# The second product of a feed-forward block as seven block products in four PSUM banks

## The chip, the cores and the metric

The kernel runs on one core of a Trainium2 chip. The metric is device time in microseconds (us) of one execution. TensorE is PE, VectorE DVE, ScalarE ACT, GpSimd POOL and SyncE SP; SP issues most of the transfers.

## What is computed

One step of a two-layer decoder: attention and a recurrent branch, a layer norm, a feed-forward block, a layer norm. What matters here is the second half of a layer:

```python
x = LN(alpha * x + mix @ w_out, ln1_g, ln1_b)           # LN1
h = square(relu(x @ w_ff_up))                           # first product: 1024 -> 4096 features
x = LN(alpha * x + h @ w_ff_down, ln2_g, ln2_b)         # second product: 4096 -> 1024, LN2
```

There are 1056 tokens (1024 of a prompt, 32 of samples), 1024 model features and 4096 inner ones, all in float32.

## The kernel before

Features lie on the partitions, tokens along the free axis in three chunks of 384, 384 and 288 columns (`CH`, chunks 0, 1 and 2). A tile is 128 features by one chunk; the model has 8 such feature tiles (`KD`), the inner layer 32. Every float32 operand is split into two parts of PE's fast float32 form: hi, a rounded copy (ACT, L287 for tokens, L236 for weights), and lo, the rest (DVE, L288 and L237). A product of two tiles is three matmuls, hi by hi, lo by hi and hi by lo, all added up in one PSUM bank (`gemm_parts`, `products`, `mmul` L206).

PE's order is written out by hand around the layer norms (`manual_schedule`); elsewhere, and on all other engines, a scheduler orders the instructions by what they depend on, and every engine works through its queue in order. `book` puts the steps of a layer norm into an agenda, at offsets counted in modelled nanoseconds of PE work (`LN_TIMES`, `LN1_TIMES`), and `weave` and `due` let them run when PE's count of issued work has got there. A layer norm has three steps on PE: the mean (a matmul of ones by the sum of the 8 tiles), the variance, and the reciprocal root brought across the partitions (`rb`, `pr`).

`ff` runs a layer's feed-forward block:
- LN1 on each chunk, in turn with the last output tiles of the branch before it. In `layer_norm` a tile is scaled on DVE (L364), gets its bias on ACT (L370), is rounded to hi on ACT, and its lo part is a subtraction on POOL (L371). The normed tile is stored in `d_x` as the residual.
- The first product: four features tile by tile (`up`), then 14 pairs of features in seven block products for chunks 0 and 1 (`pair_up`; Strassen's scheme in Winograd's form). `sums_w` makes its sums of weights on POOL (L1392 to L1395). The squared features go to DRAM (`d_h`).
- The second product: 8 groups of four features. `features` loads and splits a group's tokens (12 tiles); for each of 8 output tiles and 3 chunks, `down` adds 12 matmuls in one bank, which DVE adds to a running sum in SBUF (L1469 for the first group, L1471 for the others). Four weight loads of 512 KB go with a group.
- The last group goes chunk by chunk in hand order; `add_up` (L313) sums the finished tiles of a chunk, six adds on POOL and the last on DVE, and LN2 of chunks 0 and 1 is booked into the work that follows; LN2 of chunk 2 runs at the end.

PSUM has pools `mm` (2 banks), `pb` (4, tag `b`) and `pc` (2, tag `c`). `outer` and `inner` hold the token tiles as slots by chunk (tiles `x` and `i`), `raw` and `w` weights before and after the split.

## Time and profile before

| | |
|---|---|
| time, median of 3 runs | 3560.16 us (3554.78 to 3564.04) |
| the profiled execution | 3554.68 us, span 3552.9 us, mean granted clock 0.975 |
| busy share of the span | PE 97%, DVE 58%, ACT 33%, POOL 29% |
| second product and LN2, layer 0 | some 1395 to 1776 us |
| second product and LN2, layer 1 | some 3142 to 3553 us, with the end of the kernel |

The busy share is an average over stages. What a change of one stage does is read from that stage: the windows give the busy time of each engine in a stretch, the PE timeline what PE waited for and how long (in brackets, with the instruction that released it). The granted clock is a share of full speed. A wait on an engine that isn't the last one to be ready costs nothing.

### The profile page before, as it was taken

The numbers are of one execution on the slowest core, as the hardware profiler recorded it, in microseconds if no ns is written. First come the engines' busy times: TensorE is split into PE (matmuls) and PEld (weight loads), VectorE is DVE, ScalarE is ACT, GpSimd is POOL, SyncE is SP. The second block draws the span as 40 slices with busy tenths as digits, with TensorE's granted clock in tenths as the row PEclk, the third lists the DMA queues.
The fourth block names the chain that finished last, engine by engine and source line by source line (L and its number), as shares of the span: only waits on it lengthen the run. The fifth ranks groups of instructions, "written<-read, shape, count | busy, mean of one in ns | idle before, by whom it ended". The sixth has DMA issues, their size and how long they took to land.

```text
span 3552.9 us, 65184 instructions
## 1 busy us (share of the span) xinstructions
PE 3433.6 (97%) x24950; PEld 3177.7 (89%) x24950; DVE 2077.5 (58%) x5308; ACT 1175.9 (33%) x2677; POOL 1014.6 (29%) x1318
## 2 busy tenths in 40 slices
...
GB/s 171 49 97 114 78 76 92 77 74 191 73 67 114 98 104 206 97 95 76 19 89 44 100 106 91 77 86 79 110 171 46 87 109 110 109 197 88 90 47 50
DMA packets 282360, 342.09 MB, mean 96 GB/s; under 512 B 111168, under 2 KB 244832, under 8 KB 282016
## 3 DMA queue, kind: packets, MB, share of 16 engines
...
q0 software_dynamic: 1536, 4.52, 0.3%
...
## 4 chain that ended last, share of the span: by engine, by line
PE 82%; DVE 4%; ACT 2%; issue 2%; POOL 2%; DMA 1%; SPq 0%; ACTq 0%; POOLq 0%; DVEq 0%
PE mm L206 35%; PE b L206 25%; PE c L206 20%; PE b L210 1%; DMA d_g<-gs 1%; PE b L792 1%; PE c L210 0%; DVE pd L1018 0%; DVE x L1293 0%; DMA x<-d_h 0%; POOL x L1293 0%; DVE ln L301 0%; ACT x L370 0%; DVE ln L300 0%; POOL x L371 0%
## 5 line engine op out<-in xcount | busy, mean ns | idle before, releaser
L206 PE MATMUL mm<-x,w 128*128 128x384 f32 (+1 forms) x6630 | 1326.8, 336 | 22.9 <-ACT x L287 7.2
L206 PEld LDWEIGHTS mm<-x,w 128*128 128x128 f32 x6630 | 1082.6, 191 | 81.1 <-issue 13.0
L237 DVE TENSOR_TENSOR w<-raw,w 128x1024 fp32r<-128x1024 f32 x260 | 336.9, 1296 | 248.3 <-ACT w L236 246.2
L236 ACT CAST w<-raw 128x1024 fp32r<-128x1024 f32 x260 | 273.1, 1050 | 589.6 <-PE b L206 367.2
L206 PE MATMUL b<-x,w 128*128 128x384 f32 (+1 forms) x1958 | 457.5, 320 | 0.9 <-DVE x L288 0.9
L206 PE MATMUL mm<-i,w 128*128 128x384 f32 (+1 forms) x2034 | 425.6, 329 | 27.9 <-ACT i L287 15.6
L206 PE MATMUL c<-i,w 128*128 128x384 f32 (+1 forms) x2080 | 421.8, 323 | 3.1 <-DVE i L1308 3.0
L206 PE MATMUL b<-i,w 128*128 128x384 f32 (+1 forms) x1570 | 391.5, 324 | 3.9 <-ACT i L287 3.9
L206 PEld LDWEIGHTS mm<-i,w 128*128 128x128 f32 x2034 | 348.9, 192 | 31.6 <-ACT i L287 15.8
L206 PEld LDWEIGHTS c<-i,w 128*128 128x128 f32 x2080 | 348.4, 188 | 5.8 <-DVE i L1308 3.7
L206 PEld LDWEIGHTS b<-x,w 128*128 128x128 f32 x1958 | 334.2, 188 | 1.4 <-DVE x L288 1.4
L206 PE MATMUL c<-x,w 128*128 128x384 f32 (+1 forms) x1424 | 310.5, 323 | 0.0
L206 PEld LDWEIGHTS b<-i,w 128*128 128x128 f32 x1570 | 276.4, 188 | 4.6 <-ACT i L287 4.6
L206 PEld LDWEIGHTS c<-x,w 128*128 128x128 f32 x1424 | 242.6, 190 | 0.3 <-DVE x L288 0.3
L313 POOL TENSOR_TENSOR i<-i,i 128x384 f32<-128x384 f32 (+1 forms) x36 | 35.4, 984 | 677.6 <-DVE i L1471 673.0
L820 POOL TENSOR_TENSOR z<-z,gs 128x384 f32<-128x384 f32 (+1 forms) x84 | 80.1, 954 | 293.3 <-issue 184.5
L1471 DVE TENSOR_TENSOR i<-i,b 128x384 f32<-128x384 f32 x144 | 74.9, 520 | 144.1 <-PE b L206 143.2
L1366 POOL TENSOR_TENSOR x<-x 128x384 f32<-128x384 f32 x112 | 112.9, 1008 | 143.0 <-ACT x L1365 137.5
L1365 ACT ACTIVATE x<-x 128x384 f32<-128x384 f32 x112 | 58.6, 523 | 241.0 <-DVE x L1433 152.4
L1099 POOL COPY sav<-vt 64x128 f32<-64x128 f32 x128 | 42.9, 335 | 333.1 <-PE c L206 302.0
L313 POOL TENSOR_TENSOR i<-i,x 128x384 f32<-128x384 f32 (+1 forms) x36 | 34.7, 964 | 281.3 <-DVE x L1324 274.9
L1112 POOL TENSOR_SCALAR sd<-S,eL 128x128 f32<-128x128 f32 x128 | 96.9, 757 | 49.1 <-DVE S L1136 46.3
...
## 6 DMA issues: line engine op xcount, KB each, us to landing
...
x<-d_h SPq DMA_DIRECT2D x128, 192.0 KB
...
```

The source lines that it names most:

```text
L206: return self.nc.tensor.matmul(out, lhsT=lhsT, rhs=rhs, start=start, stop=stop)
L210: self.nc.tensor.transpose(out, x, ident)
L236: nc.scalar.copy(wf[:, 0, :], raw)
L237: self.weng.tensor_tensor(wf[:, 1, :], raw, wf[:, 0, :].bitcast(F32), op=ALU.subtract)
L313: eng.tensor_tensor(sums[c].f, a, acc[k][c].f, op=ALU.add)
L792: nc.tensor.matmul(pG[:, :n], lhsT=gup[:, pr * 128:pr * 128 + 128], rhs=z[:, :n], start=True, stop=True)
L820: nc.gpsimd.tensor_tensor(out[:, :n], out[:, :n], prev[:, :n], op=ALU.add)
L1099: nc.gpsimd.tensor_copy(sav[Kk, :], vt[Kk, k // 2, :])
L1112: nc.gpsimd.tensor_scalar(sd, S0, ecol, None, op0=ALU.mult)
L1365: nc.scalar.activation(out=z.f, in_=z.f, func=AF.Relu)
L1366: P(z.f, z.f, z.f, op=ALU.mult)
L1471: nc.vector.tensor_tensor(a, a, p[:, :n], op=ALU.add)
```

## The change

`ff` is divided into `ff_up` and `ff_down`.

**The second product** takes the tokens of chunks 0 and 1, and the even and odd features, as a 2 by 2 matrix of blocks, and the weights of even and odd features by even and odd output tiles as another. Seven block products, in the order 1, 2, 5, 4, 6, 7, 3, give the four blocks of the result. Each product runs over all 16 feature pairs in 8 steps, in four PSUM banks, one for each pair of output tiles, and is drained once, by `done`. Chunk 2 (288 columns) rides along in products 1 and 2 and in 5 and 4, in four further banks, with no product saved. For a step, `prepare` loads two token blocks of a product (and two of chunk 2), and a weight block of 512 KB, or two in product 5, which are added on POOL (L1531, into `sk`, which stays); product 6 subtracts on POOL (L1534), 7 and 3 too (L1537), 128x1024 each. Jobs are prepared two ahead.

**The first product** keeps the squared features of a pair and stores, in place of 4 tiles of 384 and 2 of 288 columns, the 7 blocks of tokens that the second product wants (`quad`, three subtractions on POOL and one on DVE) and 3 blocks of chunk 2 (`third`, one on POOL). `sums_w` goes from POOL to DVE.

**Layer norms**: hi comes straight from ACT with the bias (L375), lo from one DVE instruction with the bias (L376); the residual is made and stored after that (L387). `LN1_TIMES` are smaller. LN2 of chunk 2 is booked at the start of product 6, of chunk 0 at the start of product 3; chunk 1 comes last, and so the next layer's attention takes its keys and queries in the order 0, 2, 1. Of LN2's sums, that of chunk 1 is made by `done` in the last two products.

```diff
-LN1_TIMES = [3000, 13500, 20000]
+LN1_TIMES = [2600, 11000, 15500]
...
-                nc.scalar.activation(out=a[k], in_=a[k], func=AF.Identity, bias=bk)
-                nc.scalar.copy(hi.t, a[k])
-                nc.gpsimd.tensor_tensor(lo.t, a[k], hi.f, op=ALU.subtract)
+                nc.scalar.activation(out=hi.t, in_=a[k], func=AF.Identity, bias=bk)
+                nc.vector.scalar_tensor_tensor(lo.t, a[k], bk, hi.f, op0=ALU.add, op1=ALU.subtract)
...
+        if keep is not None:
+            for k in range(KD):
+                nc.scalar.activation(out=a[k], in_=a[k], func=AF.Identity, bias=par[:, bcol + k:bcol + k + 1])
+                nc.sync.dma_start(out=keep[k, :, c0:c0 + n], in_=a[k])
...
+        def quad(k, b11, b12, b21, b22):
+            t1, t2, t4 = [get(0, F32) for _ in range(3)]
+            P(t1.f, b12.f, b11.f, op=ALU.subtract)
+            V(b12.f, b22.f, b12.f, op=ALU.subtract)
+            P(t2.f, b22.f, t1.f, op=ALU.subtract)
+            P(t4.f, t2.f, b21.f, op=ALU.subtract)
+            for t, z in ((1, b11), (5, t1), (7, b12), (3, b22), (6, t2), (2, b21), (4, t4)):
+                store(d_t[t - 1, k], z)
...
-            P(s[0], b[0], b[1], op=ALU.add)
-            P(s[1], s[0], a[0], op=ALU.subtract)
-            P(s[2], a[0], b[0], op=ALU.subtract)
-            P(s[3], a[1], s[1], op=ALU.subtract)
+            V(s[0], b[0], b[1], op=ALU.add)
+            V(s[1], s[0], a[0], op=ALU.subtract)
+            V(s[2], a[0], b[0], op=ALU.subtract)
+            V(s[3], a[1], s[1], op=ALU.subtract)
...
+        def weights(p, k):
+            raw = lambda q: self.wraw(i["w_down"][l, q, k])
+            if p in (1, 2, 4):
+                return self.wsplit(raw({1: 0, 2: 1, 4: 3}[p]))
+            if p == 5:
+                a, b = raw(2), raw(3)
+                sk[k] = keep.tile([128, 1024], F32, tag=f"s{k}", name=self.nm("sk"))
+                P(sk[k], a, b, op=ALU.add)
+                return self.wsplit(sk[k])
+            if p == 6:
+                P(sk[k], sk[k], raw(0), op=ALU.subtract)
+                return self.wsplit(sk[k])
+            a = raw(3 if p == 7 else 1)
+            P(a, a, sk[k], op=ALU.subtract)
+            return self.wsplit(a)
...
+        def done(p, mp, e, y):
+            m = 2 * mp
+            if p == 1:
+                u[mp] = self.outer.get(0)
+                nc.scalar.copy(u[mp].f, e)
+            elif p == 2:
+                add(residual(m, 0), e)
+                P(acc[m][0].f, acc[m][0].f, u[mp].f, op=ALU.add)
+                add(residual(m, 2), y)
+            elif p == 5:
+                add(residual(m, 1), e)
+                add(residual(m + 1, 1), e)
+            elif p == 4:
+                add(residual(m + 1, 0), e, -1.0)
+                add(residual(m + 1, 2), y)
+            elif p == 6:
+                V(u[mp].f, u[mp].f, e, op=ALU.add)
+                P(acc[m][1].f, acc[m][1].f, u[mp].f, op=ALU.add)
+            elif p == 7:
+                V(u[mp].f, u[mp].f, e, op=ALU.add)
+                V(acc[m + 1][0].f, u[mp].f, acc[m + 1][0].f, op=ALU.subtract)
+                P(acc[m + 1][1].f, acc[m + 1][1].f, u[mp].f, op=ALU.add)
+                u[mp].put()
+            else:
+                V(acc[m][1].f, acc[m][1].f, e, op=ALU.add)
+                V(sums[1].f, sums[1].f, acc[m][1].f, op=ALU.add)
...
+            for q, (p, k) in enumerate(jobs):
+                if q + 2 < len(jobs):
+                    ready.append(prepare(*jobs[q + 2]))
+                if k == 0:
+                    if p in (1, 5):
+                        y = fours()
+                    e = fours() if p in (6, 3) else [self.ps(self.pb, "b") for _ in range(4)]
+                if (p, k) == (6, 0):
+                    self.book(norm(2), LN_TIMES)
+                elif (p, k) == (3, 0):
+                    self.book(norm(0), LN_TIMES)
...
+                if k == 7:
+                    for mp in range(4):
+                        done(p, mp, e[mp][:, :n], y[mp][:, :n2])
+                    for c in {4: (2,), 7: (0,)}.get(p, ()):
+                        for m in range(KD):
+                            self.add_up(inner, sums, acc, m, c)
+                    if p == 7:
+                        sums[1] = inner.get(1)
+                        P(sums[1].f, acc[1][1].f, acc[3][1].f, op=ALU.add)
+                        for m in (5, 7):
+                            P(sums[1].f, sums[1].f, acc[m][1].f, op=ALU.add)
...
-        drain(norm(2, last=True))
+        drain(norm(1, last=True))
```

The order of instructions shows what this moves, at three places of layer 0. In the rows, `x` and `i` are token tiles (chunk, slot, number), `b`, `mm` and `c` PSUM banks.

DVE in the second product before: the drains L1471 stand one by one between the splits of weights and tokens, each for a bank of its own.

```order
L1471 TENSOR_TENSOR i_1_17_2789_15738<-i_1_17_2789_15738,c_17009 128x384
L1471 TENSOR_TENSOR i_2_0_2790_15739<-i_2_0_2790_15739,b_17023 128x288
L237 TENSOR_TENSOR w_17467<-raw_17465,w_17467 128x1024
L1471 TENSOR_TENSOR i_0_11_2791_15740<-i_0_11_2791_15740,mm_17042 128x384
L1471 TENSOR_TENSOR i_1_1_2792_15741<-i_1_1_2792_15741,b_17056 128x384
L1471 TENSOR_TENSOR i_2_1_2793_15742<-i_2_1_2793_15742,c_17070 128x288
L288 TENSOR_TENSOR i_0_10_3107_17557<-x_5_3105_17554,x_3_3106_17556 128x384
```

DVE after, at the seam between product 5 and product 4: the token splits L294 are those of product 4's second step, and L1557 are the drains of product 5.

```order
L243 TENSOR_TENSOR w_18067<-raw_18065,w_18067 128x1024
L294 TENSOR_TENSOR x_1_3259_17963<-x_9_3257_17960,x_15_3258_17962 128x384
L294 TENSOR_TENSOR x_6_3262_17969<-x_11_3260_17966,x_3_3261_17968 128x384
L294 TENSOR_TENSOR x_9_3265_17975<-x_5_3263_17972,x_15_3264_17974 128x288
L294 TENSOR_TENSOR x_6_3268_17981<-x_3_3266_17978,x_8_3267_17980 128x288
L1557 SCALAR_TENSOR_TENSOR i_0_11_3249_17936<-i_0_11_3249_17936,b_17325 128x384
L1557 SCALAR_TENSOR_TENSOR i_0_15_3250_17939<-i_0_15_3250_17939,b_17325 128x384
L1557 SCALAR_TENSOR_TENSOR i_0_16_3251_17942<-i_0_16_3251_17942,b_17326 128x384
L1557 SCALAR_TENSOR_TENSOR i_0_2_3252_17945<-i_0_2_3252_17945,b_17326 128x384
L1557 SCALAR_TENSOR_TENSOR i_0_3_3253_17948<-i_0_3_3253_17948,b_17327 128x384
L1557 SCALAR_TENSOR_TENSOR i_0_19_3254_17951<-i_0_19_3254_17951,b_17327 128x384
L1557 SCALAR_TENSOR_TENSOR i_0_18_3255_17954<-i_0_18_3255_17954,b_17328 128x384
```

The drains now stand together, two for each of the four banks, and behind the four splits.

POOL before, at the end of the second product: `add_up` for chunk 0 and the first of LN2's pair sums (L348).

```order
L313 TENSOR_TENSOR i_0_17_3319_18888<-i_0_5_2773_15722,i_0_0_2776_15725 128x384
L313 TENSOR_TENSOR i_0_17_3319_18888<-i_0_17_3319_18888,i_0_1_2779_15728 128x384
L313 TENSOR_TENSOR i_0_17_3319_18888<-i_0_17_3319_18888,i_0_12_2782_15731 128x384
L313 TENSOR_TENSOR i_0_17_3319_18888<-i_0_17_3319_18888,i_0_13_2785_15734 128x384
L313 TENSOR_TENSOR i_0_17_3319_18888<-i_0_17_3319_18888,i_0_7_2788_15737 128x384
L313 TENSOR_TENSOR i_0_17_3319_18888<-i_0_17_3319_18888,i_0_11_2791_15740 128x384
L348 TENSOR_TENSOR i_0_4_3332_19005<-i_0_4_3332_19005,i_0_19_3334_19012 128x384
```

POOL after, at the seam between product 7 and product 3: the sum of chunk 0 is `i_0_17` (L319), the sum of chunk 1 `i_0_5` (L1632, L1634), and L1581 is the drain of product 7 into chunk 1.

```order
L1581 TENSOR_TENSOR i_0_15_3250_17939<-i_0_15_3250_17939,x_15_2985_16624 128x384
L1581 TENSOR_TENSOR i_0_2_3252_17945<-i_0_2_3252_17945,x_7_2986_16626 128x384
L1632 TENSOR_TENSOR i_0_5_3538_19397<-i_0_15_3250_17939,i_0_2_3252_17945 128x384
L319 TENSOR_TENSOR i_0_17_3537_19389<-i_0_1_3109_17260,i_0_6_3361_18558 128x384
L319 TENSOR_TENSOR i_0_17_3537_19389<-i_0_17_3537_19389,i_0_12_3111_17267 128x384
L1581 TENSOR_TENSOR i_0_19_3254_17951<-i_0_19_3254_17951,x_8_2987_16628 128x384
L319 TENSOR_TENSOR i_0_17_3537_19389<-i_0_17_3537_19389,i_0_9_3363_18564 128x384
L1581 TENSOR_TENSOR i_0_8_3256_17957<-i_0_8_3256_17957,x_9_2988_16630 128x384
L319 TENSOR_TENSOR i_0_17_3537_19389<-i_0_17_3537_19389,i_0_13_3113_17274 128x384
L1634 TENSOR_TENSOR i_0_5_3538_19397<-i_0_5_3538_19397,i_0_19_3254_17951 128x384
L319 TENSOR_TENSOR i_0_17_3537_19389<-i_0_17_3537_19389,i_0_4_3365_18570 128x384
L1634 TENSOR_TENSOR i_0_5_3538_19397<-i_0_5_3538_19397,i_0_8_3256_17957 128x384
```

The six adds of chunk 0's sum, which follow each other before, now stand among seven operations for chunk 1; a last one of them (L319) and then a weight subtraction (L1537) follow these rows.

POOL before, in LN1 of chunk 0: the lo parts L371, and the sums of weights L1392 to L1395.

```order
L371 TENSOR_TENSOR x_11_2317_12267<-x_1_2025_10444,x_10_2316_12266 128x384
L371 TENSOR_TENSOR x_13_2319_12274<-x_2_2026_10446,x_12_2318_12273 128x384
L371 TENSOR_TENSOR i_0_1_2321_12281<-x_3_2027_10448,x_14_2320_12280 128x384
L1392 TENSOR_TENSOR raw_12996<-raw_12994 128x512
L1393 TENSOR_TENSOR raw_12996<-raw_12996,raw_12992 128x512
L371 TENSOR_TENSOR i_0_13_2323_12288<-x_4_2028_10450,i_0_12_2322_12287 128x384
L1394 TENSOR_TENSOR raw_12997<-raw_12992,raw_12994 128x512
L371 TENSOR_TENSOR i_0_11_2325_12295<-x_5_2029_10452,i_0_7_2324_12294 128x384
```

DVE after, in the same place: the scalings L370 and the lo parts L376.

```order
L370 SCALAR_TENSOR_TENSOR x_0_2024_10447<-x_0_2024_10447,par_108,b_12215 128x384
L376 SCALAR_TENSOR_TENSOR x_7_2311_12221<-i_0_0_2023_10445,par_108,x_15_2310_12220 128x384
L370 SCALAR_TENSOR_TENSOR x_1_2025_10449<-x_1_2025_10449,par_108,b_12215 128x384
L376 SCALAR_TENSOR_TENSOR x_9_2313_12226<-x_0_2024_10447,par_108,x_8_2312_12225 128x384
L370 SCALAR_TENSOR_TENSOR x_2_2026_10451<-x_2_2026_10451,par_108,b_12215 128x384
L376 SCALAR_TENSOR_TENSOR x_11_2315_12231<-x_1_2025_10449,par_108,x_10_2314_12230 128x384
L370 SCALAR_TENSOR_TENSOR x_3_2027_10453<-x_3_2027_10453,par_108,b_12215 128x384
L376 SCALAR_TENSOR_TENSOR x_13_2317_12236<-x_2_2026_10451,par_108,x_12_2316_12235 128x384
```

The lo parts have moved from POOL's queue, where the sums of weights stood among them, to DVE's, one behind each scaling of the tile after it.

## Rows read from the trace of the kernel before

**Rows 1.** The page: busy time by engine, and the chain's shares.

```profile
PE 3433.6 (97%) x24950; PEld 3177.7 (89%) x24950; DVE 2077.5 (58%) x5308; ACT 1175.9 (33%) x2677; POOL 1014.6 (29%) x1318
...
PE 82%; DVE 4%; ACT 2%; issue 2%; POOL 2%; DMA 1%; SPq 0%; ACTq 0%; POOLq 0%; DVEq 0%
```

**Rows 2.** Windows, second product: us, busy us (count) by engine, clock, DMA.

```profile
core 0: us, PE busy (x) PEld busy (x) DVE busy (x) ACT busy (x) POOL busy (x), PEclk, DMA share, GB/s
1425.00:1725.00 300.00, 300.00 (x1879) 300.00 (x1878) 139.76 (x247) 56.15 (x91) 0.00 (x0) 1.00 0.26 83
1725.00:1776.00 51.00, 46.99 (x298) 45.68 (x297) 34.91 (x72) 16.46 (x33) 32.20 (x33) 1.00 0.03 10
```

**Rows 3.** PE timeline there: start, length, engine, line, operation, shape, count.

```profile
1410.23 2.25 PE L206 MATMUL mm<-x,w 128*128 128x384 f32 x12
1412.31 0.33 PE L206 MATMUL b<-x,w 128*128 128x384 f32 x1
```

**Rows 4.** PE timeline, stage start and LN2; in brackets wait and releaser.

```profile
1398.60 0.44 PE L206 MATMUL b<-i,w 128*128 128x384 f32 x1 [1.37 <-ACT i L287]
...
3147.15 0.44 PE L206 MATMUL b<-i,w 128*128 128x384 f32 x1 [2.57 <-ACT i L287]
...
1753.91 0.94 PE L206 MATMUL b<-ident,ln_rb 128*128 128x128 f32 x6 [1.26 <-DVE ln_rb L357]
...
1763.49 0.91 PE L206 MATMUL b<-i,ones 128*128 128x384 f32 x2 [2.62 <-DVE i L313]
```

**Rows 5.** PE windows after those waits: us, busy, clock, DMA, GB/s.

```profile
1400.00:1402.00 2.00, 2.00 (x10) 0.61 0.98 293
...
3148.00:3150.00 2.00, 2.00 (x7) 0.51 0.73 212
...
1762.00:1764.00 2.00, 0.51 (x3) 1.00 0.00 0
```

**Rows 6.** Groups by shape: count, busy us, mean ns, idle before.

```profile
L313 POOL TENSOR_TENSOR i<-i,i 128x384 f32<-128x384 f32 x24 | 24.3, 1013 | 674.4 <-DVE i L1471 672.1 <-DVE ln L301 2.0
...
L237 DVE TENSOR_TENSOR w<-raw,w 128x1024 fp32r<-128x1024 f32 x26 | 31.9, 1226 | 20.2 <-ACT w L236 20.2
...
L1471 DVE TENSOR_TENSOR i<-i,b 128x384 f32<-128x384 f32 x48 | 26.6, 553 | 53.0 <-PE b L206 52.8
...
L288 DVE TENSOR_TENSOR i<-x,x 128x384 fp32r<-128x384 f32 x14 | 7.8, 555 | 4.4 <-ACT x L287 4.3
```

**Rows 7.** Timeline in attention: POOL and DVE beside each other and alone.

```profile
1834.19 3.33 POOL L429 TENSOR_TENSOR qrot<-qrot,sin 128x1056 f32<-128x1056 f32 x1
...
1888.42 2.44 POOL L429 TENSOR_TENSOR qrot<-qrot,sin 128x1056 f32<-128x1056 f32 x1 [4.50 <-DMA qrot<-qraw]
...
1835.22 3.41 DVE L428 TENSOR_TENSOR qraw<-qraw,cos 128x1056 f32<-128x1056 f32 x1
...
1843.89 1.29 DVE L428 TENSOR_TENSOR qraw<-qraw,cos 128x1056 f32<-128x1056 f32 x1 [2.08 <-DMA qrot<-qraw]
```

**Rows 8.** A window ahead of the second product, columns as in 2.

```profile
1375.00:1400.00 25.00, 23.08 (x143) 22.50 (x142) 12.28 (x21) 11.29 (x24) 5.31 (x6) 1.00 0.90 283
```

**Rows 9.** LN1, layer 0: window (columns as in 2) and PE's waits.

```profile
1015.00:1075.00 60.00, 45.14 (x216) 40.92 (x215) 47.43 (x89) 30.40 (x64) 40.40 (x36) 0.75 0.26 87
...
1025.17 0.69 PE L206 MATMUL mm<-x,w 128*128 128x384 f32 x1 [2.22 <-ACT x L370]
...
1037.23 1.33 PE L206 MATMUL mm<-i,w 128*128 128x384 f32 x3 [3.17 <-POOL i L371]
...
1051.72 1.18 PE L206 MATMUL b<-ident,ln_rb 128*128 128x128 f32 x6 [1.97 <-DVE ln_rb L357]
...
1071.46 1.49 PE L206 MATMUL b<-ident,ln_rb 128*128 128x128 f32 x6 [5.79 <-DVE ln_rb L357]
```

**Rows 10.** PE timeline of the last LN: mean and scaling.

```profile
3524.70 0.72 PE L206 MATMUL b<-i,ones 128*128 128x288 f32 x2
...
3543.46 1.46 PE L206 MATMUL b<-ident,ln_rb 128*128 128x128 f32 x6 [2.90 <-DVE ln_rb L357]
```

173 lines of the change are left out of this document (96 added, 77 removed).

## The prediction

> **What bounds the kernel now.** I read the page's busy shares and chain first, then windows of the feed-forward stage, and then TensorE's rows inside these windows. [rows 1]: PE is busy in 97% of the span and holds 82% of the chain; no other engine is above 58%. The windows [rows 2] say the same of the second product: for 300 us PE is busy all the time at a granted clock of 1.00 (the 2.4 GHz level), DVE for 139.76 us, ACT for 56.15 and POOL not at all, and DMA moves 83 GB/s. So in this stage a matmul that is taken out is worth its full time, and the others have room. What the change puts into that room, and above all where PE has to stop for it, decides the sign.
>
> The price of a matmul: twelve products of 384 columns start at 1410.23 and the next row at 1412.31 [rows 3], so one costs 2.08/12, about 0.1735 us, while PE runs full; one of 288 columns, in proportion, 0.130.
>
> **What is removed.** Before, chunks 0 and 1 take 8 groups x 8 tiles x 2 chunks x 4 features x 3 terms = 1536 matmuls of 384 columns in each layer. After, 7 products x 8 steps x 8 weight tiles x 3 terms = 1344. Chunk 2 keeps 768 in both. So 192 go: 192 x 0.1735 = **33.3 us per layer**. Before also waits in this stage [rows 4]: at its start 1.37 us in layer 0 and 2.57 in layer 1, and in LN2 1.26 and 2.62 (layer 1's LN2 waits are a little shorter). After the start wait the granted clock falls to a mean of 0.61, and 0.51, the lower of its two levels (1.2 GHz), in layer 1's window of 2 us [rows 5]. That costs 2 x (1 - 0.61) there and about as much in the next 2 us: some 1.6 us. After the longer of the LN2 waits it stays at 1.00 [rows 5]. All of it is some **6.7 us per layer**. If every one of these waits went too, the stage would gain 40.
>
> **What is added, seam by seam.** Before drains one PSUM bank per 12 matmuls (2.08 us), the DVE add costs 0.553 [rows 6], and PE has other banks to go on with. After, one product's four banks are full at the same moment, the next product wants banks, and, as the order of the instructions shows, DVE has the drains behind the splits of the job after next. A split costs 0.555 us [rows 6], and their last cast waits for token slots that the ending product holds. I take each seam from the drains in their order:
> - 1 to 2: four copies on ACT, taken at the DVE drain's price for want of a row, the first banks used while the last are copied: 1.9.
> - 2 to 5: four DVE drains of 0.553 and what is left of a split: 3.0.
> - 5 to 4: eight DVE drains, two per bank, 8 x 0.553 = 4.4, minus what PE has to do meanwhile with the banks that come first: 4.2 with the split ahead.
> - 4 to 6: the four drains of 384 come before the four of 288, and product 6 wants the banks of the latter: 3.5.
> - LN2 of chunk 2, booked 2200 ns of PE work into product 6, waits for six POOL adds and a DVE add that start only at the seam: 3.9, and 0.8 at its reciprocal.
> - 7 to 3: LN2 of chunk 0, booked as far into product 3. Its sum stands on POOL at the end of a run of 13 adds of 384 columns, seven of which aren't its own. At 1013 ns each [rows 6] that is 13.2 us, plus 0.55 for the drain ahead and 0.56 for the last add, less 2.2 of PE work: 12.1 if nothing else is in POOL's way, 16 if a 128x1024 subtraction (2.37, from 2.44 for 1056 columns [rows 7]) has just begun and two-sided waits of about 0.5 come on top. I take 14. The wait for its variance, 1.9.
> - The start of the stage: 2, as before.
>
> The sum is 35 us per layer (25 to 42: each seam 30% shorter, or the long one at 16 and the rest 15% longer). Behind such a wait the clock may fall as it did at the stage's start, 1.6 us each for at most seven waits, or may not, as in LN2: 0 to 11, and I take 7, since most of these are longer than 2.57 [rows 4]. In products 6, 7 and 3 a step is 24 x 0.1735 = 4.16 us of PE, and POOL (2.37) and DVE (1.226 + 2 x 0.555) together 4.71: where they exclude each other they are a little late, which I price at 2 (0 to 15, the top being a rival below). Added: 35 + 7 + 2 = **44 us per layer** against 40 gained: **+4 per layer**. The cost of the other edits of the stage is nothing: weight blocks two per job in product 5 lie under 7.3 us of PE (24 x 0.1735 + 24 x 0.130), the loads of the residual stand in SP's queue ahead of their use, and if that cover fails it is the rival on loads.
>
> **LN1 and the first product.** In layer 0, between 1015 and 1075 us, PE is busy in 45.14 of 60 us at a clock of 0.75, and POOL in 40.40 [rows 9]. Its waits are 2.22 for the bias on ACT, 3.17 for the subtraction on POOL, and 1.97 and 5.79 for the reciprocals, 13.15 together. The change takes the subtraction to DVE and the hi part straight from ACT, and the weight sums from POOL, so the 3.17 goes. But the booked points come earlier too (2600, 11000, 15500 ns for 3000, 13500, 20000), which leaves 8.4 us of PE work for the mean-to-variance chain in place of 10.5, and 4.5 for the reciprocal in place of 6.5, so PE reaches the waits sooner. DVE, which had 47.43 busy us of 60, gets 24 more operations of 0.5 us in the stage. By hand I get waits of some 11 to 13 again: **-2 per layer** (-13 if all waits go, +8 if DVE's own queue makes the reciprocals late). The other stores (1776 KB per pair of features for 1056) and the extra POOL subtractions lie under about 21 us of PE per pair and cost nothing; the weight sums that go to DVE are 4 x 0.61 us there (half a 128x1024 split each [rows 6]).
>
> **The end.** The last LN is now chunk 1 alone, 384 columns wide for 288, with its sum ready early. Before, the last mean starts at 3524.70 and the last scaling at 3543.46 [rows 10]. Wider by a third on 24 DVE operations, 24 x 0.553/4: +3.3; less work of the LN before it in the way: about the same back. 0 (-4 to +4).
>
> **The sum.** 2 x (+4 - 2) + 0 = +4 against the profiled run's own 3554.7: 3559 on that scale. The median of the runs is 5.5 above the profiled one, so in medians **3564 us** from 3560.2. A difference within 0.3% (10.7 us) is what a measurement of this kernel cannot tell from none.
>
> **The rivals.**
> *Faster: POOL leaves LN1's chain for good, and the seams come out at their low end.* For it: the largest waits in [rows 9] stand on chains in which POOL takes part, and POOL is busy in two thirds of that window. Then LN1 gives up to 13 of waits, of which I count 8, per layer and not 2, and the seams cost 6 less: 2 x -12 on the forecast: **3540**. Against it: the waits for the reciprocals are counted from booked points, and these were moved up.
>
> *Slower: DVE and POOL become the bound of the last three products.* The rows show that they shut each other out: a POOL operation of 1056 columns takes 2.44 us alone and 3.33 beside a DVE one, the DVE one 1.29 alone and 3.41 beside POOL [rows 7]. Before, the second product had no POOL work at all [rows 2]. After, each step of products 6, 7 and 3 has 2.37 of POOL and 2.34 of DVE, 4.71 for 4.16 of PE. Strictly one after the other, product 7 is 8 x 0.55 = 4.4 late. Product 6 has an LN2 on top, of which I count the 8 low parts on DVE (4.4) and some 9 adds of 288 on POOL (0.75 each): 37.7 + 4.4 + 6.8 = 49 for 33.3 of PE and the 4.7 of waits that it has anyway, so 11 late. Product 3's own LN2 hides in its long wait. That makes 15 per layer and not 2: 3564 + 26 = **3590**. It decides as soon as less than an eighth of the two engines' work overlaps, since 4.71 is 1.13 times 4.16 and the jobs are prepared two ahead. The Trainium skill, page "SBUF — State Buffer", section "Who interferes with whom", states it as a rule: a DVE instruction with both inputs in SBUF and a GpSimd instruction that reads SBUF keep each other out for a whole instruction. By that rule this rival's time is the one to expect; the trace agrees as to the direction, with 3.41 for 1.29.
>
> *Slower: the loads don't keep up.* Product 5 takes 1024 KB of weights and 672 of tokens per 7.3 us, 238 GB/s; products 6, 7 and 3 take 896 KB per 4.16 us, 220. [rows 8] has 283 GB/s over 25 us with the DMA engines 90% busy, so there is room, but the whole second product before ran at 83. At 200 GB/s it would be 8 x 1.4 + 24 x 0.4 = 21 us per layer: **3605**.
>
> That the products aren't removed can be ruled out: the order of instructions on PE has them gone.
>
> **How the numbers follow.** Chances: forecast 0.38, faster rival 0.32, DVE and POOL 0.24, loads 0.06. The forecast's own bounds (seams 25 to 42, clock 0 to 11, LN1 -13 to +8) reach past 10.7 us on both sides, so of its 0.38 I give 0.04 to each side and 0.30 to no difference. Faster by over 0.3%: 0.32 + 0.04 = 0.36; within: 0.30; slower: 0.30 + 0.04 = 0.34. The range runs from 3520 (the faster rival with all LN1 waits gone and the seams at 25) to 3598; the loads' case and a tail below lie outside.
>
> **What would show it.** PE's matmul count falls by 384. Right: at product seams PE's rows wait 2 to 4 us for drains on DVE, a wait of 12 to 16 us stands on the first LN matmul of product 3 in each layer and its releaser is the sum (L319), and the clock falls behind it. The stretches inside a product are full. The faster rival: LN1's windows show under 6 us of waits. The slower: in products 6, 7 and 3 PE waits at every step for the DVE split L243, with POOL L1537 at well over 2.4. The loads: waits on DMA of raw or token blocks. I am wrong from the ground up if PE's matmul rate changes with four banks in turn, each weight used for one matmul as before, or if the long wait at 7 to 3 is absent because POOL gets there early.

## The result and the profile after

The changed kernel is slower: 3606.24 us (median of 4 runs, 3599.83 to 3609.22) against 3562.1 for the kernel before in the same series; the ratio is 1.0131, with an interval of 1.0113 to 1.0149. The forecast was 3564, the range 3520 to 3598: wrong, and the time lies above the range. The profiled execution has a span of 3603.1 us, 50.2 more than that of before.

The page of the changed kernel, its busy line and the chain's shares, answers to [rows 1]:

```profile
PE 3390.9 (94%) x24566; PEld 3129.7 (87%) x24566; DVE 2275.6 (63%) x5434; ACT 1283.5 (36%) x2869; POOL 1128.5 (31%) x1344
...
PE 69%; DVE 7%; issue 6%; POOL 5%; DMA 4%; ACT 2%; SPq 1%; POOLq 0%; ACTq 0%; DVEq 0%
```

PE has 384 matmul records fewer and 43 us less to do, as the change meant. But PE's share of the chain falls from 82% to 69%: 13 points, some 470 us, have gone over to other engines, to DMA and to issue. DVE's share of the span has risen from 58% to 63%.

Cut at the same places of the two traces (LN1's first mean, the first matmul of the second product, its last reciprocal), the 50 us lie as follows; differences of starting times, rounded, in us:

| stretch | before | after | difference |
|---|---|---|---|
| layer 0 up to LN1's first mean | 1000.8 | 989.1 | -11.6 |
| LN1 and first product, layers 0 / 1 | 393.7 / 393.8 | 393.2 / 394.0 | -0.5 / +0.2 |
| second product up to LN2's last reciprocal, layer 0 | 405.9 | 423.4 | +17.5 |
| layer 1 from there to LN1's first mean | 947.6 | 967.7 | +20.1 |
| second product to the end, layer 1 | 411.1 | 435.7 | +24.5 |

The two second products carry 42 of it, layer 1's way to LN1 the next 20. The -11.6 in the first row is not read as a gain: the code there is the same but for LN1's first booked point (0.4 us), and in the profiled executions of the changed kernel and its variants this stretch takes from 984.5 to 1015.1 us. The windows of the two second products (us, busy us and count by engine, clock, DMA share, GB/s) are the counterpart of [rows 2]:

```profile
1382.36:1805.75 423.39, 371.77 (x2253) 365.13 (x2251) 262.26 (x375) 154.31 (x276) 129.54 (x76) 0.94 0.49 160
3167.45:3603.10 435.65, 370.16 (x2210) 362.68 (x2208) 254.69 (x362) 153.96 (x276) 128.11 (x72) 0.92 0.48 155
```

PE is busy for 371.77 us in the first of them, where it had 396.70 in the same stretch before: 25 less, not 33, for the clock has gone from 0.99 to 0.94. And it stands still for 52 us, where it stood still for 9. The PE timeline of layer 0 shows where (start, length, engine, line, operation, tile, shape, count; in brackets the wait and its releaser); it answers to [rows 4]:

```profile
1390.68 1.33 PE L212 MATMUL b<-x,w 128*128 128x384 f32 x3 [5.04 <-ACT i L1469]
...
1515.95 4.18 PE L212 MATMUL b<-x,w 128*128 128x384 f32 x12 [4.38 <-DVE i L1557]
...
1644.19 1.29 PE L212 MATMUL b<-i,ones 128*128 128x288 f32 x2 [3.81 <-DVE i L319]
...
1716.70 2.18 PE L212 MATMUL b<-x,w 128*128 128x384 f32 x11 [1.39 <-DVE x L294]
...
1745.54 1.65 PE L212 MATMUL b<-i,ones 128*128 128x384 f32 x2 [23.65 <-DVE i L319]
...
1759.07 0.85 PE L212 MATMUL b<-ones,i 128*128 128x32 f32 x6 [3.56 <-DVE i L354]
...
1815.37 0.69 PE L212 MATMUL mm<-x,w 128*128 128x384 f32 x1 [8.72 <-ACT qraw L432]
```

The start of the stage costs 8 us in all (the largest of its waits, 5.04, is for a bank that ACT empties at L1469, behind casts of the new product's first blocks), the seam from product 5 to 4 4.38 (7.35 in layer 1), the mean of chunk 2's LN2 3.81. The seams from 1 to 2 and from 2 to 5 cost nothing that shows. Inside products 7 and 3 PE waits for token splits (L294) four times, 4.0 together. One wait stands above all the others: 23.65 us at the seam from product 7 to 3 (21.65 in layer 1), for the sum of chunk 0. The clock falls with it, as the windows around it show (columns as above; compare [rows 5]); 0.50 is the lower of the two levels:

```profile
1720.00:1746.00 26.00, 2.35 (x12) 2.03 (x12) 17.61 (x18) 4.57 (x8) 19.09 (x15) 0.62 0.24 79
1746.00:1748.00 2.00, 2.00 (x6) 1.39 (x6) 1.39 (x3) 0.18 (x1) 0.00 (x0) 0.50 0.17 37
```

What DVE and POOL do in these 24 us is the main reading of this case. PE has issued its twelve matmuls of product 3 by 1721.9.

```profile
1726.23 1.40 DVE L294 TENSOR_TENSOR x<-x,x 128x384 fp32r<-128x384 f32 x1 [3.71 <-ACT x L293]
1727.55 1.01 DVE L1579 TENSOR_TENSOR x<-x,b 128x384 f32<-128x384 f32 x2
...
1730.76 1.01 DVE L1579 TENSOR_TENSOR x<-x,b 128x384 f32<-128x384 f32 x2
1731.69 2.64 DVE L1580 TENSOR_TENSOR i<-x,i 128x384 f32<-128x384 f32 x2
...
1742.81 2.68 DVE L319 TENSOR_TENSOR i<-i,i 128x384 f32<-128x384 f32 x1 [4.68 <-POOL i L319]
...
1724.87 2.35 POOL L1537 TENSOR_TENSOR raw<-raw,sk 128x1024 f32<-128x1024 f32 x1 [5.97 <-DMA raw<-in_w_down_dram]
1728.17 2.26 POOL L1581 TENSOR_TENSOR i<-i,x 128x384 f32<-128x384 f32 x2 [0.96 <-DVE x L1579]
...
1741.79 0.99 POOL L319 TENSOR_TENSOR i<-i,i 128x384 f32<-128x384 f32 x1
1742.73 2.33 POOL L1537 TENSOR_TENSOR raw<-raw,sk 128x1024 f32<-128x1024 f32 x1
```

Three pieces follow each other. First, until 1728.17 nothing of the sum begins: DVE stands for 3.71 us before a token split (L294), which waits for its cast on ACT and this for a load, and the drains (L1579) are behind it in the queue. Then come POOL's 13 adds, 14.6 us. Last, the one add that DVE has in the sum (L319): it takes 2.68 us, where it takes 0.56 with nothing on POOL beside it (in the kernel with the weight sums on DVE, below), since POOL has begun a weight subtraction (L1537) 0.08 us ahead of it. DVE ends 0.43 us after POOL's 2.33 are over, and POOL's time is not lengthened. The same shows between the drains, beside POOL's adds: two L1579, which read one tile in SBUF and one bank, take 1.01 us, two L1580, which read two tiles in SBUF, take 2.64.

The load that came late has a cause of its own. SP's waits between 1660 and 1745 us (engine, line, what was waited for: us in total, times, longest):

```profile
SPq L229 <- DVE w L243: 29.4, 11, 9.4
SPq L1542 <- DVE x L294: 24.0, 11, 6.9
```

A token load (L1542) waits for the split of an earlier block; weight loads (L229) wait in the same queue for the split of an earlier weight block. The list of free slots comes round in such a way that the second block of every job gets the same slot (`x1_11` in the names of layer 0; `x_11_3260` in the order of DVE after): its load can only begin when the block of the job before has been split. Blocks are prepared two jobs ahead on paper, and one behind the other in that slot. SP asks early and waits in any case, so its waits alone don't tell what the slot costs; that was left to an experiment.

In the next layer's attention PE waits 8.72 us, the last row of the waits above. It is ACT's order (start, length, line; the first two rows are the changed kernel's):

```profile
1813.74 1.20 ACT L375 ACTIVATE x<-i,par 128x384 fp32r<-128x384 f32 x2 [1.50 <-DVE i L370]
1814.85 0.47 ACT L432 ACTIVATE qraw<-mm 128x384 f32<-128x384 f32 x1
```

```profile
1791.65 0.47 ACT L422 ACTIVATE qraw<-mm 128x384 f32<-128x384 f32 x1
...
1801.80 0.96 ACT L369 ACTIVATE i<-i,par 128x288 f32<-128x288 f32 x2 [9.31 <-DVE i L364]
```

Before, ACT empties the bank of the first keys (L422) ahead of the last norm's outputs (L369); after, the same step (L432) is behind all eight of them (L375). PE has two banks there, both full, and the tokens of two chunks lie ready for it. The first stretch of layer 1, from LN2's last reciprocal to the recurrent branch, takes 203.6 us so, for 191.2 before.

### The profile page after: what moved, and what is told of

It reads as the page before. It is cut to its first block, busy times and chain, and to the rows that moved or that the text cites. A ratio compares the mean times of both kernels' runs of the same rounds, so it can differ in the third digit from the quotient of the medians.

```text
span 3603.1 us, 65547 instructions
## 1 busy us (share of the span) xinstructions
PE 3390.9 (94%) x24566; PEld 3129.7 (87%) x24566; DVE 2275.6 (63%) x5434; ACT 1283.5 (36%) x2869; POOL 1128.5 (31%) x1344
## 4 chain that ended last, share of the span: by engine, by line
PE 69%; DVE 7%; issue 6%; POOL 5%; DMA 4%; ACT 2%; SPq 1%; POOLq 0%; ACTq 0%; DVEq 0%
PE mm L212 31%; PE b L212 18%; PE c L212 17%; DMA x<-d_t 2%; POOL x L1376 2%; DVE x L294 1%; PE b L216 1%; POOL i L319 1%; DVE w L243 1%; DMA x<-d_c 1%; PE c L216 0%; POOL x L1388 0%; ACT w L242 0%; PE b L802 0%; DVE pd L1028 0%
## 5 line engine op out<-in xcount | busy, mean ns | idle before, releaser
L212 PE MATMUL mm<-x,w 128*128 128x384 f32 (+1 forms) x7174 | 1376.8, 333 | 33.2 <-ACT qraw L432 12.5
L243 DVE TENSOR_TENSOR w<-raw,w 128x1024 fp32r<-128x1024 f32 x276 | 386.7, 1402 | 188.2 <-ACT w L242 186.0
L212 PEld LDWEIGHTS b<-x,w 128*128 128x128 f32 x2662 | 456.5, 190 | 32.9 <-ACT w L242 12.1
L212 PE MATMUL c<-x,w 128*128 128x288 f32 (+1 forms) x1968 | 364.8, 319 | 0.0
L294 DVE TENSOR_TENSOR x<-x,x 128x384 fp32r<-128x384 f32 (+1 forms) x382 | 252.1, 698 | 155.6 <-ACT x L293 151.1
L293 ACT CAST x<-x 128x384 fp32r<-128x384 f32 (+1 forms) x390 | 177.7, 483 | 387.3 <-DMA x<-d_t 240.1
L212 PE MATMUL mm<-i,w 128*128 128x384 f32 (+1 forms) x1346 | 256.2, 333 | 17.9 <-ACT i L293 16.4
L212 PE MATMUL c<-i,w 128*128 128x384 f32 (+1 forms) x1392 | 259.0, 329 | 0.0
L212 PEld LDWEIGHTS mm<-i,w 128*128 128x128 f32 x1346 | 228.8, 192 | 22.9 <-ACT i L293 17.0
L212 PEld LDWEIGHTS c<-i,w 128*128 128x128 f32 x1392 | 234.6, 190 | 0.3
L212 PE MATMUL b<-i,w 128*128 128x384 f32 (+1 forms) x770 | 158.9, 331 | 0.0
L212 PEld LDWEIGHTS b<-i,w 128*128 128x128 f32 x770 | 132.4, 188 | 0.0
L319 POOL TENSOR_TENSOR i<-i,x 128x384 f32<-128x384 f32 (+1 forms) x36 | 34.9, 969 | 305.7 <-DVE x L1334 298.9
```

What stands on the lines that cost most here:

```text
L212: return self.nc.tensor.matmul(out, lhsT=lhsT, rhs=rhs, start=start, stop=stop)
L243: self.weng.tensor_tensor(wf[:, 1, :], raw, wf[:, 0, :].bitcast(F32), op=ALU.subtract)
L293: self.nc.scalar.copy(hi, src)
L294: self.nc.vector.tensor_tensor(lo, src, hi.bitcast(F32), op=ALU.subtract)
L319: eng.tensor_tensor(sums[c].f, a, acc[k][c].f, op=ALU.add)
```

## The experiments

Theory A was that the long wait is one of booking: the mean is asked for 2.2 us into product 3, when its sum has just begun. Theory B is the rival of the prediction, DVE and POOL shutting each other out. Theory C is the slot of the token blocks. The wait in layer 1 has a theory of its own, at the end. All ratios are to the kernel before, in runs on the same chip.

### The mean asked for later

```diff
-                    self.book(norm(0), LN_TIMES)
+                    self.book(norm(0), [14000, 22000, 28000])
```

> One edit to the changed kernel: LN2 of chunk 0 is booked at 14000, 22000 and 28000 ns of PE work in product 3, in place of 2200, 9400 and 13200. Theory A (the mean is asked for too early): its sum is the last of 13 adds on POOL that begin only after product 7, so the waits of 23.65 and 21.65 us at the seam from product 7 to 3 lose their cause; with the lower clock behind them some 22 us per layer go, 3606 to about 3562 (3555 to 3575). Theory B (DVE and POOL shut each other out) and theory C (token blocks come late, since the second block of each step is loaded into the same slot): the work of product 3 is late anyway, the waits move into its steps, no more than 8 us per layer go, 3590 or more.

Measured: 3601.0 us, ratio 1.0132 (1.0106 to 1.0159). Theory A falls. The wait has gone for the most part to other rows of PE in product 3, and DVE shows why:

```profile
1737.43 1.97 PE L212 MATMUL mm<-x,w 128*128 128x384 f32 x5 [5.64 <-DVE x L294]
...
1750.19 0.69 PE L212 MATMUL mm<-x,w 128*128 128x384 f32 x1 [4.60 <-DVE x L294]
...
1770.36 1.49 PE L212 MATMUL b<-ones,i 128*128 128x32 f32 x6 [9.01 <-DVE i L354]
...
1744.70 2.70 DVE L319 TENSOR_TENSOR i<-i,i 128x384 f32<-128x384 f32 x1 [4.78 <-POOL i L319]
1747.32 2.35 DVE L243 TENSOR_TENSOR w<-raw,w 128x1024 fp32r<-128x1024 f32 x2
```

PE waits 5.64 and 4.60 for token splits and 9.01 for the variance. With 1.36 for an earlier split and 4.44 for drains at the end that is 25 us from the start of product 3 to the last norm's mean, where it was 28 (23.65, 3.56 and two small ones); in layer 1 it is 19 for 30. The ratio doesn't show it. The last add of the sum (L319) stands in DVE's queue ahead of the next weight split (L243), and it waits for POOL's adds whether PE asks for the mean or not. It is DVE's queue that holds product 3 up, and PE's order cannot go around it.

### The sum in two parts

```diff
-                P(acc[m + 1][1].f, acc[m + 1][1].f, u[mp].f, op=ALU.add)
-                u[mp].put()
+                if mp == 0:
+                    P(sums[0].f, sums[0].f, acc[1][0].f, op=ALU.add)
+                elif mp < 3:
+                    P(sums[0].f, sums[0].f, acc[m + 1][0].f, op=ALU.add)
+                else:
+                    V(sums[0].f, sums[0].f, acc[m + 1][0].f, op=ALU.add)
...
+                    if p == 5:
+                        sums[0] = inner.get(0)
+                        P(sums[0].f, acc[0][0].f, acc[2][0].f, op=ALU.add)
+                        for m in (4, 6):
+                            P(sums[0].f, sums[0].f, acc[m][0].f, op=ALU.add)
                     if p == 7:
+                        for t in range(4):
+                            P(acc[2 * t + 1][1].f, acc[2 * t + 1][1].f, u[t].f, op=ALU.add)
+                            u[t].put()
```

> One edit: the sum of chunk 0 takes its four even tiles after product 5 (they are complete since product 2) and only the four odd ones after product 7, and chunk 1's adds come behind it; the booking stays. Theory A: 3 POOL adds and one on DVE are left ahead of the mean, in place of 13; at 1.1 to 1.3 us each the wait of 23.65 falls by about 11, to 12, and as much in layer 1: 3606 to about 3582. Theory C: the drains of product 7 started 5 us after its end, since token splits stood ahead of them, so at least 8 us of wait stay whatever the sum does. Theory B: POOL does the same work in all, nothing changes outside of the seam.

Measured: 3597.9 us, ratio 1.012 (1.009 to 1.015); the gain of 0.1% cannot be told from none.

```profile
1744.95 1.65 PE L212 MATMUL b<-i,ones 128*128 128x384 f32 x2 [16.68 <-DVE i L1586]
...
1739.93 2.65 POOL L1537 TENSOR_TENSOR raw<-raw,sk 128x1024 f32<-128x1024 f32 x1
1742.55 0.98 POOL L1584 TENSOR_TENSOR i<-i,i 128x384 f32<-128x384 f32 x1
```

The wait is 16.68 and 16.25 us, 5 to 7 less. That is below what was expected, and the edit did not do all that it was meant to: POOL's order is the scheduler's, and it still put four of chunk 1's adds and a weight subtraction (L1537) ahead of and between the three adds of the sum (the last is L1584). Of the 16.68 us, 4.7 lie ahead of POOL's first add, as theory C had it, 10.6 are POOL's queue and 1.3 the last add on DVE.

### Other slots for the token blocks

```diff
-            z = self.outer.get(c)
-            nc.sync.dma_start(out=z.f, in_=src)
-            return self.parts(z, lambda: self.outer.get(c, F32R))
+            z = self.outer.get(0 if self.outer.free[0] else c)
+            hi, lo = self.outer.get(c, F32R), self.outer.get(c, F32R)
+            f = z.f[:, :CH[c][1]]
+            nc.sync.dma_start(out=f, in_=src)
+            self.split(f, hi.t, lo.t)
+            z.put()
+            return hi, lo
```

> One edit: the unsplit token blocks go into slots of chunk 0, of which 12 stand empty in the second product, and no longer through the 16 slots of their own chunk, where the second block of every step got the same slot. Theory C: loads start a step earlier or more, so PE's waits for token splits inside products 7 and 3 (4.0 and 5.6 us), the excess at the seam from 5 to 4 (3 to 6) and the 5 us ahead of product 7's drains go: 12 to 16 us per layer, 3606 to about 3577. Theory A: only the small waits go, the long one stays above 18: 3595 to 3600. Theory B: no change.

Measured: 3571.5 us, ratio 1.0045 (1.0027 to 1.0064): 31 us gained, as theory C had it. The waits inside products 7 and 3 and at the seam from 5 to 4 are gone in both layers. The long one is not:

```profile
1736.54 1.65 PE L212 MATMUL b<-i,ones 128*128 128x384 f32 x2 [22.92 <-DVE i L319]
```

So theory C is right on its part, and the 5 us ahead of the drains were not its part: with tokens there in time, the same adds and the same last add on DVE (2.68 again) make 22.92. The waits of weight loads for weight splits are still there (79.7 us of SP in this stage of layer 0, 64.9 in the changed kernel), so they are not what made PE wait inside the products. A window of product 7 shows what is left (columns as above):

```profile
1678.00:1711.00 33.00, 33.00 (x192) 33.00 (x191) 33.00 (x25) 15.84 (x24) 26.88 (x12) 1.00 0.54 170
```

DVE is busy for all of the 33 us (the time for which POOL shuts it out is in that), and so is PE. DVE falls behind, the lead covers it inside the product, and it comes out at the seam: the first drain begins 5.6 us after the product's end.

### The weight sums off POOL

```diff
-                P(sk[k], a, b, op=ALU.add)
+                V(sk[k], a, b, op=ALU.add)
...
-                P(sk[k], sk[k], raw(0), op=ALU.subtract)
+                V(sk[k], sk[k], raw(0), op=ALU.subtract)
...
-            P(a, a, sk[k], op=ALU.subtract)
+            V(a, a, sk[k], op=ALU.subtract)
```

> One edit: the 32 additions and subtractions of weight blocks (128x1024) per layer go from POOL to DVE. Theory B: with them the exclusion in products 5, 6, 7 and 3 goes, a step needs 1.2 + 1.23 + 1.1 = 3.5 us of DVE for 4.16 of PE; waits inside the steps go and POOL is free for the sums: 8 to 12 us per layer less, 3606 to about 3586. Theory A: POOL's 13 adds stay ahead of the mean, DVE has more to do ahead of the drains: no change to 5 us per layer more, 3606 to 3616.

Measured: 3558.2 us, ratio 1.0004 (0.9991 to 1.0016). One engine does more work, and 45 us go: all that the change had lost, and more than twice what was expected. The waits inside the steps and at the seam from 5 to 4 are gone here too, with the slots as they were, and the long one is shorter. DVE is no longer full in product 7:

```profile
1728.95 1.65 PE L212 MATMUL b<-i,ones 128*128 128x384 f32 x2 [15.43 <-DVE i L319]
...
1678.00:1711.00 33.00, 33.00 (x192) 33.00 (x192) 30.95 (x38) 15.66 (x24) 5.49 (x4) 1.00 0.69 221
```

The first drain begins 1 us after the product's end, and the last add takes 0.56 us; POOL's 13 adds make up the rest of the wait.

This is theory B's side, but it leaves two readings open: POOL's running as such, or the 2.4 us that POOL stands between a block's landing and its split. Two kernels tell them apart.

### No weight sums, and weight sums to the side

```diff
             if p == 5:
                 a, b = raw(2), raw(3)
                 sk[k] = keep.tile([128, 1024], F32, tag=f"s{k}", name=self.nm("sk"))
-                P(sk[k], a, b, op=ALU.add)
-                return self.wsplit(sk[k])
+                return self.wsplit(a)
...
-                P(sk[k], sk[k], raw(0), op=ALU.subtract)
-                return self.wsplit(sk[k])
+                return self.wsplit(raw(0))
...
-            P(a, a, sk[k], op=ALU.subtract)
```

> The changed kernel with the 32 additions and subtractions of weight blocks per layer left out, so that products 5, 6, 7 and 3 take weight blocks as they are loaded (the result is not the reference's). Theory B: what counts is that POOL does not run beside DVE; without these instructions nothing is left to collide, and DVE has 1.2 us per step less than where it took them over: 3545 to 3558, a little below the 3558 of that run. If DVE's own load counted there, this comes out 15 us or more below it.

The second keeps POOL's instruction on each landed block, into a tile that is read by nobody that counts:

```diff
-                P(sk[k], a, b, op=ALU.add)
-                return self.wsplit(sk[k])
+                P(sk[0], a, b, op=ALU.add)
+                return self.wsplit(a)
...
-                P(sk[k], sk[k], raw(0), op=ALU.subtract)
-                return self.wsplit(sk[k])
+                a = raw(0)
+                P(sk[0], sk[1], a, op=ALU.subtract)
+                return self.wsplit(a)
...
-            P(a, a, sk[k], op=ALU.subtract)
+            P(sk[0], a, sk[1], op=ALU.subtract)
```

> As the run with the weight sums left out, but POOL still runs an addition or subtraction of 128x1024 on each loaded block, into a tile that nobody reads; the split takes the loaded block without waiting for it (the result is not the reference's). Theory B1, exclusion: POOL's running alone holds DVE's splits up; the time stays near the changed kernel, 3590 to 3610. Theory B2, the chain: it is the 2.4 us of POOL between a block's landing and its split that make the weights late; without them in the way the time falls to 3545 to 3565 though POOL is as busy.

Measured: 3559.1 us without them (ratio 1.0003, 0.9985 to 1.0021), 3623.2 with them to the side (1.0172, 1.0146 to 1.0198). With no split waiting for POOL's result, the time is 64 us above the same kernel without POOL's instructions, and not below the changed kernel (0.4% above it by the ratios, whose intervals just overlap). So the chain is not the cause, and POOL's running is. DVE's groups by shape in the second product of layer 0 (count, busy us, mean ns, idle before and its releaser) show it in the splits, first without, then with POOL at work:

```profile
L243 DVE TENSOR_TENSOR w<-raw,w 128x1024 fp32r<-128x1024 f32 x56 | 72.3, 1292 | 102.2 <-ACT w L242 102.1
...
L294 DVE TENSOR_TENSOR x<-x,x 128x384 fp32r<-128x384 f32 x108 | 61.3, 598 | 31.8 <-ACT x L293 31.7
```

```profile
L243 DVE TENSOR_TENSOR w<-raw,w 128x1024 fp32r<-128x1024 f32 x55 | 82.5, 1501 | 89.9 <-ACT w L242 89.7
L294 DVE TENSOR_TENSOR x<-x,x 128x384 fp32r<-128x384 f32 x108 | 76.8, 745 | 26.4 <-ACT x L293 26.3
```

The same splits take 1501 ns for 1292 and 745 for 598, some 27 us more in this layer: exclusion. One thing besides still waits for POOL in this kernel, a load into a block that POOL is reading (19.8 us of SP's waits in this stage, 22.0 in the changed kernel); which part of the 64 us it has was not told apart. That DVE's own load doesn't count here shows in the run without weight sums: it has 32 instructions of 1.2 us fewer per layer than the run with them on DVE, and the same time.

### The edits together

The booking, the sum in two parts, the slots and the weight sums, with the diffs shown above; of each one line:

```diff
+                    self.book(norm(0), [14000, 22000, 28000])
...
+                        P(sums[0].f, acc[0][0].f, acc[2][0].f, op=ALU.add)
...
+            z = self.outer.get(0 if self.outer.free[0] else c)
...
+                V(sk[k], a, b, op=ALU.add)
```

> The four edits together: weight sums on DVE, unsplit tokens through chunk 0's slots, the sum of chunk 0 in two parts with chunk 1's adds behind it, and LN2 of chunk 0 booked at 14000, 22000 and 28000 ns in product 3. If the causes are separate, the 15.4 us at the seam 7 to 3 that the weight sums on DVE leave, 3.7 at the variance and some small waits go: 15 to 20 us per layer on 3558, 3520 to 3530, below the kernel before. If the late booking still finds product 3's steps late, as it did alone, it gains under 5 per layer: 3548 to 3558.

Measured: 3532.2 us, ratio 0.9928 (0.9904 to 0.9953): faster than the kernel before, and just above the 3520 to 3530 expected. In the second product of layer 0 (of a profiled execution that took 3551.1 us, the longest of the seven) PE's share is 367.33 us of 388 at a clock of 0.98. Left is a wait for the variance, and drains at the end of product 3 (4.45):

```profile
1406.00:1794.00 388.00, 367.33 (x2272) 364.21 (x2270) 257.32 (x402) 156.16 (x272) 45.51 (x44) 0.98 0.55 175
...
1756.72 1.49 PE L212 MATMUL b<-ones,i 128*128 128x32 f32 x6 [7.73 <-DVE i L354]
```

Three variants say what the parts are worth beside each other. The first has the weight sums on DVE and one line more:

```diff
-                    self.book(norm(0), LN_TIMES)
+                    self.book(norm(0), [14000, 22000, 28000])
```

> Weight sums on DVE and the late booking of LN2 of chunk 0, without the two other edits. The late booking alone moved the wait into product 3's steps and gained 5 us. If that was because POOL's 13 adds and 8 subtractions held product 3's splits up, then with the subtractions off POOL the 15.5 us per layer at the seam go for the most part: 3558 to about 3535. If the adds alone hold the splits up, the wait comes back in the steps again: 3550 or more.

Measured: 3556.9 us, 0.9984 (0.9965 to 1.0002). The 15.4 us at the seam come back as 5.85 for a split and 8.00 for the variance, so the adds do hold the splits up, by DVE's last add of the sum in its queue; without the two other edits the booking is worth nothing here either.

The second has the four edits with the weight sums back on POOL:

```diff
-                V(sk[k], a, b, op=ALU.add)
+                P(sk[k], a, b, op=ALU.add)
...
-                V(sk[k], sk[k], raw(0), op=ALU.subtract)
+                P(sk[k], sk[k], raw(0), op=ALU.subtract)
...
-            V(a, a, sk[k], op=ALU.subtract)
+            P(a, a, sk[k], op=ALU.subtract)
```

> The run with the four edits, but the weight sums back on POOL: slots of chunk 0, the sum in two parts, the late booking. It tells what the exclusion costs once the token loads have room. If room alone makes up for it (POOL's and DVE's 4.71 us per step overlap enough, as the slots run had it, whose waits inside the steps were gone), this comes out with the four edits, 3525 to 3540. If the exclusion sets the pace of product 3, where the sums of LN2 run on POOL as well, the waits come back there as 5 to 10 us per layer: 3545 to 3560.

Measured: 3545.7 us, 0.9971 (0.9958 to 0.9983). With room in the slots the exclusion costs 0.43%, 15 us, and for the most part it costs it in product 3, where PE waits 6.43 and 5.25 us for splits:

```profile
1721.62 0.69 PE L212 MATMUL mm<-x,w 128*128 128x384 f32 x1 [6.43 <-DVE x L294]
```

The third has the four edits and LN1 of chunk 2 booked later:

```diff
+LN1_TIMES_2 = [8000, 16000, 25000]
...
-                                      keep=self.d_x[l]), LN1_TIMES)
+                                      keep=self.d_x[l]), LN1_TIMES if c < 2 else LN1_TIMES_2)
```

> The same, and LN1 of chunk 2 booked at 8000, 16000 and 25000 ns in place of 2600, 11000 and 15500. PE waits there 5.3 us for the mean and 8.2 for the reciprocal in each layer, while two chunks of the next product stand ready. If these are waits of booking alone, 10 to 13 us per layer go: 3497 to 3510. If DVE's queue is what is late, the waits come back in the first features of the next product: under 5 per layer.

Measured: 3522.2 us, 0.9892 (0.9867 to 0.9917). The intervals of this and of the four edits overlap. In the trace LN1's waits of more than 1 us fall from 5.30, 2.15 and 8.20 to two of 7.37 and 2.92, so 5 us per layer, less than expected.

```profile
1036.00 1.62 PE L213 MATMUL b<-ident,ln_rb 128*128 128x128 f32 x6 [7.37 <-DVE ln_rb L364]
```

On top of that, the mean of LN2 earlier and its other two points later:

```diff
-                    self.book(norm(0), [14000, 22000, 28000])
+                    self.book(norm(0), [10000, 25500, 31000])
```

> The four edits and LN1 of chunk 2 booked later, with LN2 of chunk 0 at 10000, 25500 and 31000 ns in place of 14000, 22000 and 28000: PE waited 6.9 and 6.5 us for the variance there and had no wait for the mean. The chain from mean to variance takes 8 + 6.9 = 15 us, so 15.5 of PE work between them should cover it: 10 us in all, 3522 to about 3512. If the chain is longer because it starts beside POOL's adds, the wait stays above 4: 3517 to 3522. The reciprocal at 31 us leaves the end of product 3 little room: up to 4 per layer may come back there.

Measured: 3527.0 us, 0.9889 (0.9861 to 0.9917), no different. The wait for the variance fell from 6.86 to 1.06, and the end of product 3 took a part of it back: 2.90 us at the last LN's reciprocal in layer 0, where it was 1.60, and 6.19 in front of the last mean in layer 1, where it was 3.72. In all, PE's waits from the variance to that reciprocal are 7.9 us for 13.1 in layer 0 and 12.5 for 14.5 in layer 1; the time doesn't show these 7 us.

Whether LN1's booking is worth something by itself, the kernel before can tell:

```diff
+LN1_TIMES_2 = [8000, 18500, 27000]
...
-                                      keep=self.d_x[l]), LN1_TIMES)
+                                      keep=self.d_x[l]), LN1_TIMES if c < 2 else LN1_TIMES_2)
```

> The kernel before with one edit: LN1 of chunk 2 is booked at 8000, 18500 and 27000 ns in place of 3000, 13500 and 20000. Its wait of 5.8 us for the reciprocal of that chunk and the slow clock behind it go if it is a booking matter: 6 to 9 us per layer, 3558 to about 3544. If the other waits of LN1 grow instead (3.2 for the subtraction on POOL, 2.0 for the reciprocal of chunk 1), under 3 per layer: within 0.3%. It tells whether this gain belongs to the change or to any kernel of this form.

Measured: 3562.3 us, 1.0002 (0.998 to 1.0024), nothing. The 5.8 us for the reciprocal are gone, and in their place PE waits for the lo parts from POOL, 2.21, 1.18 and 1.47, a little later:

```profile
1062.14 0.80 PE L207 MATMUL mm<-x,w 128*128 128x384 f32 x3 [2.21 <-POOL x L372]
```

### More banks at the handover to layer 1

```diff
+            if l:
+                self.gbanks.append((self.pc, "c"))
             gk, gq = keys(), queries(0)
...
             drain(gq)
+            self.gbanks = deque([(self.mm, "mm")])
```

> The changed kernel, with four PSUM banks in place of two for the first projections of layer 1's attention (keys, values and queries of each chunk), as long as the last LN2 of layer 0 runs. If ACT's order makes the wait of 8.72 us there, through the two full banks: by the order of the instructions PE has 15 more matmuls of 384 columns and 24 of 288 before it needs ACT, 15 x 0.174 + 24 x 0.130 = 5.7 us, and nine more go into the wait for the reciprocal (1.95). Then the wait falls to about 3, layer 1's first stretch gets 6 to 9 us shorter, and the time is about 3599, ratio 1.011. If PE there waits for chunk 1's outputs in any case (they are ready at about the time when the wait ends), the wait stays within 1 us or comes back before PE's first matmuls of chunk 1, and the ratio stays at 1.013. The intervals of the two will overlap; PE's rows of the trace decide.

Measured: 3602.7 us, ratio 1.013 (1.0107 to 1.0153). In the trace PE now issues its 15 and 24 matmuls while ACT writes the norm's outputs, and the wait for the same step of ACT is 2.92, as ACT's order through the full banks had it:

```profile
1805.75 2.85 PE L212 MATMUL mm<-x,w 128*128 128x384 f32 x15
1808.44 3.36 PE L212 MATMUL c<-x,w 128*128 128x288 f32 x24
1814.72 0.61 PE L212 MATMUL mm<-x,w 128*128 128x288 f32 x1 [2.92 <-ACT qraw L432]
```

The wait for the reciprocal ahead of it goes from 1.95 to 0.39, and the stretch to the recurrent branch from 203.6 to 195.9 us, so 9 are gained there, and nothing stands in front of chunk 1's first matmuls. In the time it doesn't show. The interval reaches from 8 us below the changed kernel's ratio to 8 above, and the single runs of the same kernel, 3591 to 3605, lie further apart than the gain.

> The same four banks on top of the four edits and LN1 booked later (0.9892, 3522.2). If ACT's order is the cause: 6 to 9 us less, 3514, ratio 0.987. If not, 0.989.

Measured: 3524.7 us, 0.9909 (0.9889 to 0.993), where it was 0.9892 without the banks; the intervals overlap. The wait is 2.51 for 8.66, and the stretch 196.4 for 203.8, so the trace has the same gain here as well. What takes it back in the time is not settled. The next stretch, to LN1's first mean, took 768.6 us in this profiled run and 765.5 without the banks, where before took 756.4; the clock's falls, of which the last section tells, are in these numbers.

The best kernels of the series, then, are the changed one with the four edits and LN1 booked later, with or without the later points of LN2 and the banks: 0.9 to 1.1% below the kernel before.

## Why the prediction was wrong

**What bounds, and the saving: right.** 384 matmuls are gone, and every one was worth its time while PE ran full. PE's busy time in layer 0's second product fell by 25 us and not by 33 because the clock's loss is in it.

**The seams, the step that failed.** The sum of 35 us per layer came out at 49.5 and 49.8, with 4.0 and 5.8 in it for waits inside products 7 and 3, which were to be full. Its parts were wrong in both directions. The largest, the seam from 7 to 3, was priced at 14 (12 to 16) and measured 23.65 and 21.65. Its working had the 13 adds (13.2 us, measured 14.6), but it let POOL begin 0.55 us after the product's end. In the trace of layer 0 POOL begins 9.3 us after it, since weight splits, and token splits of which one waits for a load, stand in DVE's queue ahead of the drains. And it put 0.56 for the last add on DVE, which took 2.68 beside POOL's subtraction. The start was priced at 2 and measured 8.1 and 5.3, the variance at 1.9 and measured 4.5 and 4.8. The seams 1 to 2, 2 to 5 and 4 to 6 were priced at 8.4 and cost 0.84 or less: there PE gets its banks in time. The mean of chunk 2 was priced at 3.9 and measured 3.81 and 3.83, which is right. The seam 5 to 4 was priced at 4.2 for its eight drains and measured 4.38 and 7.35; that 4.38 is so near is luck, since with other slots, or with the weight sums on DVE, the same eight drains cost PE nothing there. The remark that the last cast of a job waits for slots was in the text; that one slot makes each load wait for the split before it was not seen, and giving the blocks other slots took 31 us away. The bound of 42 for this sum was also added up wrongly: 16, and the rest 15% longer, make 40.

**DVE and POOL: the rival whose cause came true, by another path.** It was given a chance of 0.24 and 3590. Its cause is shown: POOL's instructions, whose results nobody reads, cost 64 us. Its path was that PE waits at every step of products 6, 7 and 3 for the weight split. PE waits at four of these steps in layer 0, for token splits, 4.0 us together, and with other slots at none, though DVE is then full in product 7. What DVE is behind comes out at the seam. So the price failed in the sentence that product 3's LN2 hides in its long wait: the long wait is itself lengthened by the two engines taking turns, from 15.43 us with the weight sums on DVE to 23.65. And 2 us per layer were put into the forecast for exclusion, as if overlap could be counted on. The weight sums on POOL cost the changed kernel 45 us in both layers; with the other slots, the sum in two parts and the late booking they cost 15.

The Trainium skill's page "SBUF — State Buffer", section "Who interferes with whom", says that a DVE instruction with two inputs in SBUF and a GpSimd instruction that reads SBUF exclude each other for the whole instruction, whichever comes first. The trace agrees, with 2.68 us for an add of 0.56 that began 0.08 after POOL's. In the prediction that rule stood behind a rival; these runs would have put it into the forecast's sum.

**The clock: about right in layer 0.** Priced at 7 us per layer (0 to 11); the stretch of layer 0 runs at 0.94 for 0.99 and shows 25 us saved where 33 were due, 8. In layer 1 the stretch holds the end of the kernel too. It runs at 0.92 for 0.96, and PE's busy time falls from 389.73 to 370.16 us, so 14 are lost there.

**LN1 and the first product: LN1 right in size, in part by luck.** -2 per layer was forecast. Measured -2.8 and -2.4 in LN1 with the first four features, and +2.3 and +2.6 in the pairs, which had been priced at nothing, so -0.5 and +0.2 for the whole. The waits were to be 11 to 13 and are 16.4 in layer 0, 14.8 before; the stretch is shorter even so because PE is busy for 81.1 us in place of 85.4, at a clock of 0.89 for 0.85. The largest waits moved as the text said: 5.30 for the mean of chunk 2 and 8.21 for its reciprocal, in place of those of [rows 9].

```profile
1022.39 1.30 PE L212 MATMUL b<-i,ones 128*128 128x288 f32 x2 [5.30 <-DVE i L319]
...
1051.71 1.46 PE L212 MATMUL b<-ident,ln_rb 128*128 128x128 f32 x6 [8.21 <-DVE ln_rb L363]
```

**The end: within its bounds.** 0 was forecast (-4 to +4). From the last mean to the last scaling it takes 15.3 us, where [rows 10] have 18.8.

**Not seen at all: the next layer's attention.** 12 us in layer 1, of which 8.72 is one wait. Chunk 1 as the last one changes ACT's order at the handover, and the prediction stopped at the stage's end. All variants of the changed kernel have this wait, at 8.66 to 9.01, but the two with more banks, 2.92 and 2.51; that it comes from ACT's order through two full banks is shown in the trace, and what it is worth in the time of the whole kernel could not be told from the scatter.

**The loads** were priced as a matter of bandwidth, which they are not. With the weight sums on DVE, product 7 moves 221 GB/s with PE full, which is what the text said it needs; where loads came late they had been asked for late. That this rival's 3605 lies next to the measured time is luck.
